# A hybrid token-mixer step: the scan is begun beside the last group's block inverse

## The chip, the cores and the metric

The kernel runs on one core of a Trainium2 chip. The metric is device time in microseconds (us) of one execution. TensorE (PE) does matrix products; VectorE (DVE), ScalarE (ACT) and GpSimd (POOL) work on tiles; SyncE (SP) issues most of the transfers, and ACT and POOL issue some. Each engine takes its instructions in order.

## The reference

One layer of a flow-matching backbone for 2048 sample tokens and 128 prompt tokens, D = 1024. The input is modulated and normalised, then projected once (`w_in`), and the columns are shared among three branches, which are gated and merged, and projected once more. The branch that the change touches is a gated DeltaNet, run in both directions:

```python
m = eye + bc[..., :, None] * jnp.einsum('bnhik,bnhjk->bnhij', kc, kc) * dec_strict
rhs = jnp.concatenate([vc * bc[..., None], kc * (bc * jnp.exp(gam))[..., None]], axis=-1)
sol = lax.linalg.triangular_solve(m, rhs, left_side=True, lower=True, unit_diagonal=True)
...
def step(s, inp):
    u0_, w_, qk_, qg_, kd_, gl_ = inp
    u = u0_ - jnp.einsum('bhck,bhkv->bhcv', w_, s)
    o = jnp.einsum('bhck,bhkv->bhcv', qg_, s) + jnp.einsum('bhij,bhjv->bhiv', qk_, u)
    s = gl_[..., None, None] * s + jnp.einsum('bhck,bhcv->bhkv', kd_, u)
    return s, o
```

The other branches are a spatial gating unit (SGU) and a Fourier mixer. All output is float32.

## The kernel before

Operands are split into a high and a low half-precision part, and each product is made of three matmuls (`mm3`, and `gemm_T` and `gemm_N` for the projections; all are recorded at L250, in the helper `mm`). Tokens are worked on in blocks of 512, 512, 512, 512 and 128 (`TBS`), or in 17 chunks of 128.

The stages follow one another on TensorE: modulation and normalisation; the columns for q, k and v with a short convolution; the SGU; the Fourier branch in four groups of columns, g = 0 to 3 (the projection, whose results are split into `xc` at L1571 and L1572; `columns_of`, `rows_in`, `rows_out`; the gates at L1454 to L1468, whose products `st` POOL makes at L1466 and stores at L1468); three merges, each with a gate and a branch projection for eight blocks of 128 output columns (L1690 loads the branch's blocks into `two`); and the output projection. Weights come through two buffers `wst`, loaded at L291 by SP.

The DeltaNet branch runs beside the SGU, the Fourier branch and the merges. It is a Python generator, `delta()`, that is advanced between pieces of the other stages: each piece adds to an account (`pace.tick`), and for each `QUOTA` of 1.6 units in it the generator goes on to its next `yield`. With scan the quota becomes `SCAN`. A unit is about a microsecond of TensorE's work. A scheduler then fixes each engine's order from the order of the code, from priorities and from its own estimate of times.

`delta()` does this:

- It prepares the 17 chunks one after another (`prep`), in five groups: [16], [0 to 3], [4 to 7], [8 to 11], [12 to 15]. The groups are numbered 0 to 4 here. For each chunk a triangular matrix is stored to DRAM (`nd`, issued by POOL at L1074).
- Beside the chunks of a group, `base_inverse` works on the group before it. It loads all 32x32 diagonal blocks of the group into `XB` (L1103), brings them into order with a copy on DVE (L1107), and inverts them in a chain of 31 steps. In each, DVE makes a product (L1114) and POOL subtracts it from `E` (L1115), and each waits for the other. ACT and DVE split the result in two (L1122, L1123), and it is stored to DRAM as `ei` of the group: groups 0 to 3 by SP at L1431 and by ACT at L1003; group 4 by SP at L1130 and by ACT at L1131.
- Group 4 has no chunks of another group beside it: it is worked on alone, to its end, in 27 slices.
- Then the pool `dqa` with all tiles of this part is closed, and a pool `dqb` takes its room. The tiles of the new pool cannot be written before the last readers of the old one have ended, stores included.
- `scan()` goes through 34 steps (chunk 16, then 0 to 15; and 16, then 15 to 0), some 12 slices each. A step's `level()` assembles the inverse of a chunk from its 32x32 blocks: it loads `ES` (L1171, three loads, from `ei`) and `N3` (L1175), both with one buffer, and `sn` (L1177); the first products are `ES` by `N3`; ACT and DVE split them into `Q3` (L1184 to L1186), POOL copies blocks from `ES` into `T16` and `R16` (L1188, L1190), and three more rounds of products follow. The buffers are cleared once by POOL (L1137). The chain of states S follows, with loads of `skn`, `sv`, `sk` and `sqk` (L1268 to L1322), and the output of a chunk (`attend`, `finish`: transposes at L1382, a store to `br`). Between its first loads and its first products scan lets 14 slices go by.

The merge of the DeltaNet branch is the last of the three, so that scan has until then to end.

## Time and profile before

| what | us |
|---|---|
| median of 3 runs (2136.2 to 2143.67) | 2139.85 |
| the profiled execution, its own time | 2138.49 |
| its span in the profile | 2136.7 |
| TensorE busy in the span | 2081.9 |

The granted clock of TensorE is 0.991 of full speed on average. In the rows below, a line such as L1114 is a line of the kernel before, and `out<-in` are the program's names without their buffer numbers. "SPq" is an engine's queue of transfers. A time in brackets behind an instruction is how long its engine had been idle, and what ended that. Where matmuls follow one another, a row gives the start of each and a length in which neighbours overlap.

### The profile page before, as it was taken

What the parts mean: (1) busy time and instruction counts of PE and PEld (TensorE: products, weight loads), DVE (VectorE), ACT (ScalarE), POOL (GpSimd) and SP (SyncE); (2) the same over time, 40 slices, a digit from 0 to 9 for tenths busy, and PEclk for the clock granted to TensorE, in tenths of its full rate; (3) what the DMA queues carried; (4) which work ended last, traced back from release to release, by engine and by line L of the source; (5) the groups of instructions that cost most, each with busy time, mean ns of one, the idle gap of its engine ahead of it and who ended that gap; (6) DMA issues with size and microseconds to landing.
All of it is one profiled execution on the core that took longest, in us unless ns stands there. A gap on an engine that the chain in (4) does not pass through costs nothing.

```text
span 2136.7 us, 42553 instructions
## 1 busy us (share of the span) xinstructions
PE 2081.9 (97%) x16133; PEld 1196.5 (56%) x16133; DVE 1326.9 (62%) x2945; ACT 1059.7 (50%) x2456; POOL 844.5 (40%) x1089
## 2 busy tenths in 40 slices
PE   7999999999999999989999999999999999999998
PEld 4454444455555678778565556565655444444443
DVE  6656854379777786556755555866665554666245
ACT  5554744465665664445644445765653443453112
POOL 0321332225465554543321233355542234333464
PEclk9999999999999999999999999999999999999999
DMA  9525722177767744444655555767764644456862
GB/s 354 221 78 188 271 103 103 62 222 232 254 222 247 217 162 133 110 133 128 228 178 168 168 162 185 236 203 233 210 207 131 218 163 165 173 193 236 343 221 89
DMA packets 222286, 403.24 MB, mean 189 GB/s; under 512 B 39225, under 2 KB 109137, under 8 KB 219265
## 3 DMA queue, kind: packets, MB, share of 16 engines
q1 hardware_dynamic: 167040, 290.58, 42.3%
q0 software_dynamic: 15216, 65.89, 8.2%
q10 hardware_dynamic: 39824, 44.05, 6.0%
q8 instruction: 127, 2.08, 0.4%
q14 instruction: 79, 0.64, 0.1%
HBM read 258.19 MB, written 142.24 MB: 187 GB/s over the span
## 4 chain that ended last, share of the span: by engine, by line
PE 53%; DVE 7%; DMA 5%; POOL 4%; ACT 3%; issue 3%; SPq 0%; ACTq 0%; POOLq 0%; DVEq 0%
PE b L250 52%; POOL E L1115 1%; DMA tw<-tw 1%; DVE XB L1114 1%; POOL st L1466 1%; DMA sqk<-qk 1%; DMA ei<-XB 1%; ACT nd L1066 0%; DMA wst<-in_w_blk_dram 0%; DVE XB L1123 0%; PE b L1382 0%; POOL ss L1024 0%; DMA br<-st 0%; DMA skn<-kv 0%; DVE xh L182 0%
## 5 line engine op out<-in xcount | busy, mean ns | idle before, releaser
L250 PE MATMUL b<-xh,whi 128*128 128x512 f16 (+1 forms) x1920 | 651.0, 348 | 1.7 <-DVE sg L1456 1.6
L250 PE MATMUL b<-xl,whi 128*128 128x512 f16 (+1 forms) x1920 | 651.1, 348 | 0.0
L250 PE MATMUL b<-xh,wlo 128*128 128x512 f16 (+1 forms) x1920 | 650.2, 347 | 0.0
L250 PEld LDWEIGHTS <-whi 128*128 128x128 f16 x3856 | 352.5, 98 | 324.8 <-issue 6.1
L250 PEld LDWEIGHTS <-wlo 128*128 128x128 f16 x1928 | 188.8, 98 | 175.8 <-issue 1.8
L250 PE MATMUL b<-big,bhi 128*128 128x512 f16 (+1 forms) x960 | 250.2, 347 | 0.1
L250 PE MATMUL b<-big,blo 128*128 128x512 f16 (+1 forms) x480 | 163.1, 347 | 0.0
L1739 POOL TENSOR_TENSOR mrow<-mrow,sg 128x512 f32<-128x512 f32 (+1 forms) x80 | 95.3, 1193 | 127.7 <-DVE sg L1738 103.4
L953 POOL TENSOR_TENSOR cy<-cy,raw 128x545 f32<-128x545 f32 (+1 forms) x48 | 65.5, 1390 | 182.7 <-ACT raw L952 182.7
L250 PEld LDWEIGHTS <-xh 128*128 128x128 f16 x1496 | 117.0, 98 | 29.0 <-issue 1.5
L250 PEld LDWEIGHTS <-bhi 128*128 128x128 f16 x960 | 87.5, 98 | 76.7 <-issue 0.2
L1115 POOL TENSOR_TENSOR E<-E,XB 128x31 f32<-128x31 f32 (+15 forms) x155 | 94.6, 610 | 85.3 <-DVE XB L1114 68.6
L250 PEld LDWEIGHTS <-xl 128*128 128x128 f16 x1068 | 98.1, 98 | 45.9 <-DMA tw<-tw 2.4
L1729 ACT ACTIVATE sg<-b,winv 128x512 f32<-128x512 f32 (+1 forms) x120 | 74.0, 617 | 93.4 <-PE b L250 92.4
L1188 POOL COPY T<-ES 32x256 f16<-32x256 f16 x68 | 31.9, 470 | 177.0 <-DMA ES<-ei 144.6
L250 PE MATMUL b<-whi,xh 128*128 128x128 f16 x544 | 92.8, 219 | 0.0
L250 PE MATMUL b<-whi,xl 128*128 128x128 f16 x544 | 92.8, 219 | 0.0
L250 PE MATMUL b<-wlo,xh 128*128 128x128 f16 x544 | 92.8, 219 | 0.0
L328 DVE SCALAR_TENSOR_TENSOR wlo<-wst,wsc,whi 128x1024 f16<-128x1024 f32 x52 | 71.0, 1368 | 30.2 <-ACT whi L327 29.0
L1295 POOL TENSOR_TENSOR skn<-skn,ed 128x512 f32<-128x512 f32 x34 | 37.1, 1090 | 112.6 <-DMA skn<-kv 112.6
L1114 DVE TENSOR_TENSOR XB<-XB,E 128x31 f32<-128x31 f32 (+15 forms) x155 | 54.3, 350 | 41.8 <-POOL E L1115 41.2
L315 ACT ACTIVATE wlo<-wst 128x1024 f16<-128x1024 f32 x52 | 54.8, 1055 | 50.5 <-DMA wst<-in_w_blk_dram 47.2
(531 smaller groups left out, 4315.0 us busy)
## 6 DMA issues: line engine op xcount, KB each, us to landing
wst<-in_w_blk_dram SPq DMA_DIRECT2D x58, 512.0 KB, 5.0
pa<-pa POOLq DMA_DIRECT2D x16, 896.0 KB, 4.6
qkv<-cy POOLq DMA_DIRECT2D x12, 1089.0 KB, 5.3
two<-br SPq DMA_DIRECT2D x24, 512.0 KB, 5.9
mrow<-mrg SPq DMA_DIRECT2D x16, 576.0 KB, 5.1
pa<-pa SPq DMA_DIRECT2D x5, 1792.0 KB
dc<-dec SPq DMA_DIRECT2D x17, 512.0 KB, 4.7
kq<-qkv SPq DMA_DIRECT2D x34, 256.0 KB, 4.7
```

The source lines that it names most:

```text
L250: newest[0] = PE.matmul(out, l, r, start=start, stop=stop, skip_group_check=reopened)
L315: w.squared = A.activation(w.lo, st, AF.Square, accum_out=ss)
L328: w.low = V.scalar_tensor_tensor(w.lo, st, s, w.hi, ALU.mult, ALU.subtract)
L953: G.tensor_tensor(y[:, c0:c1], y[:, c0:c1], raw[:, 1 + c0:1 + c1], ALU.mult)
L1114: V.tensor_tensor(t3, X3[:, 0:k, k:k + 1].to_broadcast([P, k, n_]), E3[:, k:k + 1, k:32].to_broadcast([P, k, n_]), ALU.mult)
L1115: G.tensor_tensor(E3[:, 0:k, k:32], E3[:, 0:k, k:32], t3, ALU.subtract)
L1188: G.tensor_copy(T16[rows(a0, b), :, :, b], ES[0:32, :, 2 * a0 + b, :, wT])
L1295: G.tensor_tensor(h3(kn_), h3(kn_), bc(ed[:, d, t, :], P), ALU.mult)
L1466: G.tensor_tensor(o, sg, src, ALU.mult)
L1729: gated_[0] = A.activation(sg, ps, AF.Sigmoid, scale=gw.inv)
L1739: G.tensor_tensor(mr, mr, sg, ALU.add)
```

## The change

Group 4's inverse gets a pool of its own, `lastp`, opened with the pool of the Fourier branch and closed with it; its room is used by the merges' pools afterwards. `delta()` issues group 4's loads (eight steps of the generator) and takes one slice for them, then closes `dqa`, opens `dqb` and begins scan. With every second slice of scan, group 4's inverse goes on by one step of its generator, which is two of its 31 steps. The first of its two stores for each half is issued by POOL instead of SP; ACT still issues the second. `SCAN` goes from 1.3 to 1.42.

```diff
-SCAN = 1.3
+SCAN = 1.42
...
-        XB = sb(dq, [P, 2048], "XB")
+        own = dq if g < 4 else lastp[0]
+        XB = sb(own, [P, 2048], "XB")
         X, tmp = XB[:, 0:1024], XB[:, 1024:2048]
-        E = sb(dq, [P, 1024], "E")
+        E = sb(own, [P, 1024], "E")
...
             else:
-                SY.dma_start(*out[0])
+                G.dma_start(*out[0])
                 A.dma_start(*out[1])
...
         for o_ in extra:
             SY.dma_start(*o_)
-        for _ in base_inverse(4):
-            yield 1
+        base = base_inverse(4)
+        for _ in range(8):
+            next(base)
+        yield 1
         dl.close()
         dq = pool(dl, "dqb", 1, side="right")
...
         pace.quota, pace.fine = SCAN, True
-        yield from scan()
+        for i_, _ in enumerate(scan()):
+            if i_ % 2:
+                next(base, 0)
+            yield 1
         dl.close()
...
     fp = pool(fs, "fp", 1)
+    lastp.append(pool(fs, "lastp", 1))
```

Lines behind L1093 move by one, and those of the Fourier branch and the merges by six or seven: L1114 is L1115 in the changed kernel, L1123 is L1124, L1456 is L1462, L1572 is L1579.

TensorE, in the second group of the Fourier branch, row 10871 on, before. `b_10081` is a projection's last tile; `xc_10043` is the split result of the one before it:

```order
10871 L250 MATMUL b_10081<-wlo_8406,xh_94 128x128
10872 L250 LDWEIGHTS xl_95
10873 L250 MATMUL b_10081<-whi_8405,xl_95 128x128
10874 L250 LDWEIGHTS xc_10043
10875 L250 MATMUL b_10109<-cf_1308,xc_10043 128x128
```

And now, where `b_10124` is the same projection:

```order
10871 L250 MATMUL b_10124<-wlo_8409,xh_94 128x128
10872 L250 LDWEIGHTS xl_95
10873 L250 MATMUL b_10124<-whi_8408,xl_95 128x128
10874 L250 LDWEIGHTS N_1229_9715
10875 L250 MATMUL b_10149<-ES_9717,N_1229_9715 128x32
```

The first products of scan stand in row 10875, behind the same projection and with as many rows ahead of them as the `xc` product had; before, they stood in row 12387.

DVE at the end of group 3's inverse, before (`XB_7998` and `E_7999` are group 3's; `sg` and `yT` belong to the Fourier branch's output, `xc_9671` to its next group):

```order
886 L1641 TENSOR_TENSOR yT_8301<-b_9397,us_9422 128x8x32
887 L1642 TENSOR_TENSOR yT_8301<-b_9397,us_9422 128x8x32
888 L1114 TENSOR_TENSOR XB_7998<-XB_7998,E_7999 128x60
889 L1456 SCALAR_TENSOR_TENSOR sg_9492<-b_9467,zs_8303,sg_9492 128x512
890 L264 CAST wscb_10126<-wss_10063 128x1
891 L1456 SCALAR_TENSOR_TENSOR sg_9561<-b_9536,zs_8303,sg_9561 128x128
892 L1114 TENSOR_TENSOR XB_7998<-XB_7998,E_7999 128x31
893 L1572 SCALAR_TENSOR_TENSOR xc_9671<-b_9574,xc_9671 128x512
894 L1123 SCALAR_TENSOR_TENSOR XB_7998<-E_7999,XB_7998 128x16x32 x4
```

And now (`XB_9692` and `E_9693` are group 4's, `xc_9674` is the tile that was `xc_9671`):

```order
886 L1108 COPY XB_9692<-XB_9692 64x1024
887 L1115 TENSOR_TENSOR XB_7998<-XB_7998,E_7999 128x60
888 L1462 SCALAR_TENSOR_TENSOR sg_9495<-b_9470,zs_8306,sg_9495 128x512
889 L1648 TENSOR_TENSOR yT_8304<-b_9400,us_9425 128x8x32
890 L1649 TENSOR_TENSOR yT_8304<-b_9400,us_9425 128x8x32
891 L1115 TENSOR_TENSOR XB_9692<-XB_9692,E_9693 128x31
892 L1115 TENSOR_TENSOR XB_7998<-XB_7998,E_7999 128x31
893 L264 CAST wscb_10187<-wss_10122 128x1
894 L1462 SCALAR_TENSOR_TENSOR sg_9564<-b_9539,zs_8306,sg_9564 128x128
895 L1115 TENSOR_TENSOR XB_9692<-XB_9692,E_9693 128x60
896 L1124 SCALAR_TENSOR_TENSOR XB_7998<-E_7999,XB_7998 128x16x32 x4
897 L1579 SCALAR_TENSOR_TENSOR xc_9674<-b_9577,xc_9674 128x512
```

Group 4's copy has moved ahead of group 3's last two steps, and the split of `xc` has moved behind group 3's four conversions. POOL's order moves with it: its three products `st` stand ahead of group 3's last step, where two steps stood behind them before; its clearing of scan's buffers stands behind six steps of group 4, and the other 25 stand between scan's copies.

More of the change, by code (lines that the diff above doesn't have):

```diff
@@ L1129, in base_inverse @@
             else:
-                SY.dma_start(*out[0])
+                G.dma_start(*out[0])
                 A.dma_start(*out[1])
-    odd, wide, q_st, q_hi = [1], [], [], []
+    odd, wide, q_st, q_hi, lastp = [1], [], [], [], []
     def zeroed(cols, tag):
```

## The prediction

> **What bounds the kernel now.** I read the page first, then TensorE's busy time by stretches of 10 us, then what it waited for in the stretches that stand out. The page's line of engines:
>
> ```profile
> PE 2081.9 (97%) x16133; PEld 1196.5 (56%) x16133; DVE 1326.9 (62%) x2945; ACT 1059.7 (50%) x2456; POOL 844.5 (40%) x1089
> ```
>
> TensorE is the bound, and the change takes no matmul away. So it can move the time only through TensorE's idle time and through the stretches in which its clock is granted at half. The stretches where that stands (start:end, length, then busy time by engine, granted clock, DMA share, GB/s):
>
> ```profile
> 890.00:900.00 10.00, 9.29 (x142) 8.06 (x140) 3.15 (x7) 3.40 (x8) 7.76 (x9) 1.00 0.83 243
> 900.00:910.00 10.00, 8.56 (x61) 4.31 (x59) 4.16 (x10) 3.45 (x6) 5.05 (x8) 1.00 0.49 144
> 910.00:920.00 10.00, 6.17 (x77) 5.10 (x74) 4.93 (x15) 4.62 (x14) 3.55 (x9) 0.75 0.32 85
> 920.00:930.00 10.00, 10.00 (x114) 7.07 (x112) 4.97 (x11) 4.16 (x12) 4.61 (x9) 0.91 0.36 116
> 930.00:940.00 10.00, 7.27 (x133) 6.83 (x131) 9.50 (x25) 5.15 (x15) 4.11 (x7) 1.00 0.67 197
> 1030.00:1040.00 10.00, 5.68 (x67) 4.77 (x63) 6.72 (x20) 8.36 (x21) 4.57 (x6) 0.72 0.81 275
> 1040.00:1050.00 10.00, 10.00 (x56) 4.78 (x55) 6.58 (x14) 6.13 (x13) 1.23 (x1) 0.94 0.91 329
> 1350.00:1400.00 50.00, 47.88 (x414) 27.96 (x413) 36.13 (x90) 34.14 (x91) 20.11 (x24) 1.00 0.77 237
> 1050.00:1650.00 600.00, 596.39 (x5302) 354.72 (x5301) 368.42 (x940) 318.76 (x837) 219.60 (x291) 1.00 0.62 191
> ```
>
> From 890 to 940 TensorE is idle for 0.71 + 1.44 + 3.83 + 2.73 = 8.7 us, and clocks of 0.75 and 0.91 cost 2.5 + 0.9 = 3.4 us more: 12.1 us. This is where scan begins. At 1030 to 1050, where the merges begin, the same reckoning gives 4.3 + 3.4 = 7.7 us. In the 600 us after that, through which scan runs on, only 3.6 us are idle. What TensorE waited for, first from 900 to 960, then from 1020 to 1060 (us in total, times, longest):
>
> ```profile
> PE b L250 <- DMA ES<-ei: 4.1, 2, 2.3
> PE b L250 <- DMA N<-n: 1.4, 1, 1.4
> PE b L250 <- ACT Q L1186: 1.0, 1, 1.0
> PE b L250 <- DVE X L1627: 0.8, 1, 0.8
> PE b L250 <- ACT R L1203: 0.5, 1, 0.5
> ```
>
> ```profile
> PE b L250 <- DVE Q L1219: 1.5, 1, 1.5
> PE b L250 <- DVE o L1248: 1.3, 1, 1.3
> PE b L250 <- DVE S L1232: 0.8, 1, 0.8
> PE b L250 <- ACT S L1231: 0.7, 1, 0.7
> ```
>
> The first list is scan's start: the loads of ES and N, which nothing has fetched ahead. SyncE's queue and the time line say why (start, us, engine, line, operation):
>
> ```profile
> SPq L1130 <- DVE XB L1123: 36.8, 1, 36.8
> ```
>
> ```profile
> 883.31 2.24 SPq L1130 DMA_DIRECT2D ei<-XB  x2
> 888.56 0.33 SPq L291 DMA_DIRECT2D wst<-in_w_blk_dram  x1
> 890.81 0.33 SPq L1270 DMA_DIRECT2D skn<-kv  x1
> 896.83 2.77 SPq L1171 DMA_DIRECT2D ES<-ei  x3
> ```
>
> ```profile
> 890.86 0.95 POOL L1137 MEMSET R<- 128x1024 f16 x1 [9.54 <-DVE Y L1572]
> 901.82 1.75 POOL L1188 COPY T<-ES 32x256 f16<-32x256 f16 x2 [3.19 <-DMA ES<-ei]
> ```
>
> ```profile
> 902.43 0.18 PE L250 MATMUL b<-ES,N 128*128 128x32 f16 x1 [1.44 <-DMA N<-n]
> 902.46 0.38 PE L250 MATMUL b<-xh,whi 128*128 128x512 f16 x1
> 902.67 0.28 PE L250 MATMUL b<-ES,N 128*128 128x32 f16 x5
> ```
>
> The store of group 4's inverse blocks SyncE for 36.8 us. When it has landed, near 890.8, its room goes to scan, and GpSimd's clearing and SyncE's loads begin together. The first product of scan comes at 902.43, **11.6 us after the landing**.
>
> **The change part by part.** The sum is made against the profiled execution, 2138.49 us, which is 1.4 us under the median of the three runs.
>
> *Scan's start leaves 900.* Scan's first room is now the one that group 3 frees. In the order, its first product stands in row 10875 of TensorE, where before the first `cf,xc` product of that place stood. This row gives the time of it:
>
> ```profile
> 838.13 0.28 PE L250 MATMUL b<-cf,xc 128*128 128x128 f16 x2
> ```
>
> So scan starts 64 us earlier on TensorE. Counted over the order's rows at 0.21 us for 512 columns (from 902.46 to 902.67 above), the first products of scan's steps now stand 22, 17, 18 and 19 us of TensorE's work apart, and stood 8.5, 10.7 and 7.3 apart. ES has one buffer, and one turn of clearing or freeing, loading and using it took the 11.6 us above: the old spacing is under that, the new one over it. The waits on ES and N go, and the weight load at 888.56, which was held up behind the store, is free. I take the whole 12.1 us off, and put 1.5 us back for the waits on ACT's Q and R, which are inside a step and come with it: **-10.6 us**.
>
> *Group 3's inverse ends later.* DVE now copies group 4's matrix ahead of group 3's last steps. The rows for it:
>
> ```profile
> 806.85 0.78 POOL L1074 DMA_DIRECT2D nd<-nd  x1 [0.68 <-ACT nd L1066]
> DMA to landing us min/median/max: 2.3/2.6/4.1
> 813.32 3.73 POOL L1466 TENSOR_TENSOR st<-sg,yT 128x512 f32<-128x512 f32 x3 [1.74 <-DVE XB L1114]
> 818.95 0.26 POOL L1115 TENSOR_TENSOR E<-E,XB 128x31 f32<-128x31 f32 x1
> 824.69 1.95 SPq L1431 DMA_DIRECT2D ei<-XB  x2
> 836.09 1.05 DVE L1107 COPY XB<-XB 64x1024 f32<-64x1024 f32 x1 [3.81 <-DMA XB<-nd]
> 824.03 0.28 PE L250 MATMUL b<-cf,xc 128*128 128x128 f16 x2
> ```
>
> (The second row is the landing time of the stores and loads of `nd`.) The store of 806.85 lands near 809.5; the load behind it takes up to 4.1 us, so near 814. DVE, in order, sits before the copy until then, copies for 1.05 us, does group 3's last step but one and two output products (near 817.2). GpSimd has put its three products of 3.73 us ahead of its last step, which therefore ends near 821.4 and not at 819.2. From that end to the store of 824.69, group 3's conversions took 5.5 us, so they now end near 826.9. DVE and ACT have them ahead of the split of `xc` (0.7 us more), which TensorE wants at 824.03: **a wait of 3.6 us** that was not there.
>
> *Scan's first room comes late.* The landing times of the stores and loads of `ei` from 800 to 905:
>
> ```profile
> DMA to landing us min/median/max: 5.3/5.7/5.9
> ```
>
> Group 3's second store went out at about 825.4, within the row of 824.69; it goes out 2.2 us later and lands up to 5.9 us after that, near 833.5. With the 11.6 us above the first product can begin at 845.2. TensorE gets there at 838.13 + 3.6 = 841.7: **another 3.6 us**. The two together put TensorE **7.2 us** back. Bounds: 2 us if DVE's copy comes in time, 11 us if GpSimd, which has six of group 4's steps ahead of the clearing, is late too. I take 7.2, since each term has its own row. While GpSimd waits for the landing, DVE waits with it for group 4's next step, and behind that stand splits of `xc`; TensorE wants these only after scan's first product, so they cost 0. So does the weight load that stands behind the same landing on SyncE, which is read later still.
>
> Behind these two waits the clock may fall to half. Between 910 and 920 it did after 3.8 us of idle time in several pieces. In 1350:1400, 2.1 us of idle time left it at 1.00. The new waits lie just short of the first. The Trainium skill, "TensorE: Matmul & The Clock Gate" (section "What's actually happening"), says that the clock falls to half after an idle window of about 3.4 us, and that the window runs free; by that rule one of the new waits can, but need not, hold a whole window. If the first does it, the second wait is filled by the slower work and the sum is unchanged. If the second does, it costs the 3.4 us of the two older cases; by that rule alone the sum would be 3.4 us higher at most. The trace agrees with it as far as it goes: both half-clock stretches follow idle time of about that size, though in pieces.
>
> *Group 4's inverse beside scan.* Its row in the stretch from 830 to 882 (ns, min/median/max):
>
> ```profile
> L1115 POOL TENSOR_TENSOR E<-E,XB x31: 247/587/1597, 837.5 to 880.0; 128x31 f32<-128x31 f32 x2, 128x60 f32<-128x60 f32 x2, 128x87 f32<-128x87 f32 x2, 128x112 f32<-128x112 f32 x2
> ```
>
> These 31 steps took 43 us with GpSimd nearly to themselves. Now 25 of them stand between scan's copies, which wait for loads. The order puts the last nine behind the fourth step's T copies, so that the store goes out some 60 us of TensorE's work after scan's start, and one ES load stands behind `two` on SyncE, which waits for that store. I count 2 to 3 us in hand: **0**; gone, it costs what the store is late beyond that. Two issues on GpSimd in place of SyncE cost 0.8 us each by the row of 806.85; GpSimd is 40% busy: 0.
>
> *The merges' start.* Scan's step there is another one, the crowd of operations the same. Bounds: -7.7 (all goes) to +3.4 (a second half-clock stretch). I take **-1.5**: one of the four waits above.
>
> *Wider steps.* 431 slices of 0.12 units more are 52 us of TensorE's work, against an earlier start of 42 (26 slices of 1.6) in the pace's units: the last step ends about 10 us later. By the order's rows scan's last transposes then stand 5 us of TensorE's work ahead of the last block that needs them, against 17 before. In the 600 us with 3.6 us idle the steps stand further apart. Bounds -3.6 to +3; I take **-1.5**.
>
> The sum: -10.6 + 7.2 + 0 - 1.5 - 1.5 = -6.4, so 2138.5 - 6.4 = **2132 us**. Against the median this is -0.37%. About 0.3%, 6.4 us, is what a measurement of this kernel can tell from no change: faster means under 2133.4.
>
> **The rivals.**
>
> *The gain is eaten on the way (same).* The new waits cost the clock (+3.4), and the merges give nothing back: -10.6 + 7.2 + 3.4 = 0, so 2138.5; with half of it, 2135. For it: two waits of 3.6 us only 14 us apart. Against it: the spacing of scan's steps removes the old waits in any case. Chance 0.33.
>
> *GpSimd's queue makes group 4 late (slower).* Each of the 25 steps waits behind scan's copies, which themselves wait for loads. If each takes 0.6 us longer, as long as one takes now, the store is 15 us late; less 2.5 in hand, TensorE waits 12.5 us at `two`'s ES load, with half clock 16: 2132 + 16 = 2148. It decides where TensorE loses 14 us to it, so from 13 us late on. For it: at its start scan's T copy has waited 3.2 us for ES (901.82). Against it: with the steps 17 us apart these loads are there early. The Trainium skill speaks for this rival ("Trainium Architecture — The Big Picture", section "What this means for kernel authors", which says that VectorE and GpSimd share a pair of ports as an exclusive lock): scan's two-input work on DVE would stretch group 4's steps on GpSimd. The maximum of 1597 ns against 587 in the row above may be such a case; 25 of them would be 25 us. Chance 0.15.
>
> *The change does more than I think (faster).* Group 3's end does not slip, and the merges' start is clean: -10.6 + 2 - 7.7 - 3 = -19, 2119. Chance 0.1, within "faster".
>
> **How the numbers follow.** The forecast has 0.42 and the better case 0.1, so faster has 0.52; same 0.33; slower 0.15. The likeliest case is 2132. The range goes from 2121, 2 us short of the better case, to 2144, midway between the eaten gain and the slower case: it leaves out half of the better case and nearly all of the slower one, some 0.2.
>
> **What would show it right or wrong.** Right: the waits on `ES<-ei` near 900 are gone and the clock there is 1.00; TensorE waits for `xc` near 824 and for ES or N near 842, 7 us together; the first product of scan begins near 845; SyncE has no wait of 36.8 us. Wrong: a half-clock stretch between 825 and 860; a wait of GpSimd for `XB` and of SyncE at `two` near 910; or waits on ES that are still there in scan's first four steps, which would mean that the spacing was not the cause.

## The result, and the profile after

| | before | after |
|---|---|---|
| median of 5 runs each, one chip, us | 2137.75 | 2151.12 |
| lowest and highest, us | 2133.26, 2143.67 | 2148.17, 2155.43 |
| the profiled execution, its own time, us | 2138.49 | 2148.17 |
| its span, us | 2136.7 | 2146.4 |

The ratio of after to before is 1.0064, with an interval of 1.0040 to 1.0088: the changed kernel is slower by 13 to 14 us, where a gain of 6 us was forecast. The profiled execution is the fastest of the five and shows 9.7 us of it. TensorE's line on the page after:

```profile
PE 2086.3 (97%) x16133; PEld 1197.9 (56%) x16133; DVE 1327.7 (62%) x2945; ACT 1060.5 (49%) x2456; POOL 850.0 (40%) x1091
```

The matmuls are as many as before (16133). TensorE's busy time grew by 4.4 us and its span by 9.7, so that the rest, 5.3 us, is idle time. Busy time can grow without more matmuls where the clock is lower, since each then takes longer. To see where, I cut the span where the kernel's work changes: 800 to 890 (the second group of the Fourier branch, where scan now begins), 890 to 960 (where scan began), 960 to 1020, 1020 to 1070 (the merges' start), 1070 to 1640 (scan runs on). Before, then after; the columns are those of the prediction's stretches:

```profile
800.00:890.00 90.00, 88.32 (x1172) 72.83 (x1172) 57.48 (x136) 41.36 (x88) 44.28 (x72) 0.97 0.38 109
890.00:960.00 70.00, 61.29 (x819) 48.53 (x817) 37.19 (x93) 30.07 (x76) 34.70 (x53) 0.95 0.49 148
960.00:1020.00 60.00, 58.62 (x845) 47.63 (x843) 39.05 (x106) 30.91 (x81) 20.47 (x37) 1.00 0.46 142
1020.00:1070.00 50.00, 45.68 (x365) 26.54 (x364) 37.00 (x96) 32.50 (x72) 18.93 (x25) 0.93 0.68 230
1070.00:1640.00 570.00, 566.39 (x5098) 339.12 (x5096) 345.85 (x886) 301.66 (x796) 211.15 (x281) 1.00 0.62 191
```

```profile
800.00:890.00 90.00, 81.75 (x1062) 65.70 (x1061) 54.78 (x133) 41.18 (x95) 54.25 (x86) 0.94 0.44 130
890.00:960.00 70.00, 64.54 (x870) 50.50 (x868) 46.40 (x120) 34.59 (x84) 25.36 (x46) 0.95 0.56 163
960.00:1020.00 60.00, 60.00 (x911) 51.35 (x909) 38.59 (x96) 30.48 (x75) 24.23 (x36) 1.00 0.43 134
1020.00:1070.00 50.00, 42.59 (x439) 28.34 (x437) 37.78 (x102) 31.91 (x78) 23.43 (x32) 0.90 0.65 210
1070.00:1640.00 570.00, 564.87 (x4952) 334.12 (x4951) 338.64 (x860) 293.18 (x760) 204.76 (x267) 1.00 0.60 186
```

Of each row, the length less PE's busy time is idle, and the length times what the clock lacks of 1.00 is lost to the clock. The two together, as the prediction reckoned them (us; the clock's two digits leave up to 0.5 us open in a row):

| stretch | before | after | difference | forecast |
|---|---|---|---|---|
| 800 to 890 | 1.7 + 2.7 = 4.4 | 8.2 + 5.4 = 13.6 | +9.2 | +7.2 |
| 890 to 960 | 8.7 + 3.5 = 12.2 | 5.5 + 3.5 = 9.0 | -3.2 | -10.6 |
| 960 to 1020 | 1.4 | 0.0 | -1.4 | 0 |
| 1020 to 1070 | 4.3 + 3.5 = 7.8 | 7.4 + 5.0 = 12.4 | +4.6 | -1.5 |
| 1070 to 1640 | 3.6 | 5.1 | +1.5 | -1.5 |
| sum | 29.4 | 40.1 | +10.7 | -6.4 |

The sum of the differences, 10.7, stands against 9.7 us of span; 4.2 of it go to the clock, about the 4.4 us by which TensorE's busy time grew. The last column has the prediction's terms. Its first term holds 1.5 us of waits for Q and R that move with scan's start, so by place it forecast +8.7 and -12.1. The new place costs about what was forecast, the old place gives back less than a third of what was forecast, and the merges' start costs where it should have gained. The waits of TensorE in the three places (us in total, times, longest), first from 805 to 880:

```profile
PE b L250 <- DVE sg L1462: 2.9, 1, 2.9
PE b L250 <- DMA N<-n: 2.2, 1, 2.2
```

then from 880 to 960:

```profile
PE b L250 <- DMA ES<-ei: 2.4, 1, 2.4
PE b L250 <- ACT S L1232: 1.0, 1, 1.0
```

and from 1020 to 1075:

```profile
PE b L250 <- ACT S L1232: 5.4, 2, 5.2
```

The first two are the two waits of the term +7.2. Their chain can be followed in the time line of the changed kernel:

```profile
813.89 1.03 DVE L1108 COPY XB<-XB 64x1024 f32<-64x1024 f32 x1 [2.19 <-DMA XB<-nd]
...
815.89 0.22 PE L250 MATMUL b<-whi,xh 128*128 128x128 f16 x1 [2.87 <-DVE sg L1462]
...
832.88 0.95 POOL L1138 MEMSET R<- 128x1024 f16 x1 [0.26 <-DMA ei<-XB]
...
843.75 0.46 PE L250 MATMUL b<-ES,N 128*128 128x32 f16 x8 [2.20 <-DMA N<-n]
```

DVE sits for 2.19 us before the copy of group 4 until its load has landed at 813.89, and TensorE waits for the `sg` product behind it. Group 3's store lands at 832.88; GpSimd then clears, SyncE loads, and the first product of scan comes at 843.75, 10.9 us after the landing. The second place, 880 to 960, in SyncE's queue and the time line:

```profile
SPq L1697 <- DMA ei<-XB: 5.4, 1, 5.4
```

```profile
912.75 0.84 POOL L1131 DMA_DIRECT2D ei<-XB  x1 [0.42 <-DVE XB L1124]
...
921.40 1.41 SPq L1697 DMA_DIRECT2D two<-br  x3
922.91 0.41 SPq L1273 DMA_DIRECT2D sv<-kv  x1
923.36 0.48 SPq L1172 DMA_DIRECT2D ES<-ei  x1
...
929.24 0.43 PE L250 MATMUL b<-ES,N 128*128 128x32 f16 x8 [2.38 <-DMA ES<-ei]
```

The 36.8 us wait of SyncE is gone, but the loads of `two` take the room of group 4's inverse and now wait 5.4 us for its store. The last of three ES loads stands behind them, goes out at 923.36, and TensorE waits for it. This is scan's fifth step; the first four begin at 843.75, 867.88, 888.91 and 907.53, and from the second on none waits for ES or N. The place cut at 920 and 940 shows it:

```profile
890.00:920.00 30.00, 30.00 (x485) 26.72 (x483) 19.52 (x46) 17.07 (x37) 12.79 (x25) 1.00 0.58 164
920.00:940.00 20.00, 16.13 (x120) 9.07 (x118) 10.13 (x28) 5.66 (x13) 4.71 (x8) 0.83 0.56 179
```

Up to 920, where the kernel before lost most of its 12.2 us, nothing is lost any more. From 920 to 940 it is 3.9 us of idle time and 3.4 of clock. The third place, first in SyncE's queue:

```profile
SPq L1273 <- DVE binv L1712: 10.6, 1, 10.6
```

```profile
1041.07 0.68 DVE L1233 SCALAR_TENSOR_TENSOR u<-sv,u 128x512 f16<-128x512 f32 x1
...
1041.77 0.32 SPq L1273 DMA_DIRECT2D sv<-kv  x1
...
1043.00 0.33 SPq L291 DMA_DIRECT2D wst<-in_w_brb_dram  x1
...
1046.35 0.63 ACT L315 ACTIVATE blo<-wst 128x512 f16<-128x512 f32 x1 [4.32 <-DMA wst<-in_w_brb_dram]
...
1049.90 0.61 ACT L1232 ACTIVATE S<-S 128x512 f16<-128x512 f32 x1
```

A load of `sv` holds SyncE's queue for 10.6 us, and the branch's weight load stands behind it. The view names `binv`, which came last, but `binv` does not touch `sv`; the buffer is read by DVE's u, which ends as the load goes out. ACT waits 4.32 us for the weights with its split of S behind that, and TensorE waits 5.2 us for S.

### The profile page after: what moved, and what is told of

It reads as the page before. It is cut to its first block, busy times and chain, and to the rows that moved or that the text cites. A ratio compares the mean times of both kernels' runs of the same rounds, so it can differ in the third digit from the quotient of the medians.

```text
span 2146.4 us, 42529 instructions
## 1 busy us (share of the span) xinstructions
PE 2086.3 (97%) x16133; PEld 1197.9 (56%) x16133; DVE 1327.7 (62%) x2945; ACT 1060.5 (49%) x2456; POOL 850.0 (40%) x1091
## 5 line engine op out<-in xcount | busy, mean ns | idle before, releaser
L327 ACT ACTIVATE whi<-wst,wsc 128x1024 f16<-128x1024 f32 x52 | 59.3, 1142 | 41.6 <-DVE wsc L278 41.6
L1115 DVE TENSOR_TENSOR XB<-XB,E 128x31 f32<-128x31 f32 (+15 forms) x155 | 56.2, 363 | 38.2 <-POOL E L1116 37.6
```

What stands on the lines that cost most here:

```text
L327: w.made = A.activation(w.hi, st, AF.Copy, scale=s)
L1115: V.tensor_tensor(t3, X3[:, 0:k, k:k + 1].to_broadcast([P, k, n_]), E3[:, k:k + 1, k:32].to_broadcast([P, k, n_]), ALU.mult)
```

## The experiments

The theory after the result (S in the expectations): the waits of scan's start were not removed by moving it. They went to the next place where a load comes late. Three were named above: scan's first products ahead of their room, and on SyncE's queue ES behind `two` and the weights behind `sv`. The rivals: the wider quota by itself is what costs; the place of the store's issue (GpSimd's queue) costs; group 4's chain beside scan costs wherever it stands. All ratios are to the kernel before on the same chip, with a 95% interval; its median was 2141.2 to 2141.9 us, so 0.1% is 2.1 us.

**The quota alone** (`e1_spacing_1_3`, the changed kernel; `e4_before_1_42`, the kernel before):

```diff
-SCAN = 1.42
+SCAN = 1.3
```

```diff
-SCAN = 1.3
+SCAN = 1.42
```

> The changed kernel with scan's quota back at 1.3; all else is as changed. Theory S (three separate places: group 3's late end and scan's late room near 820 to 850, 7 us; scan's fourth and fifth steps, where the ES load stands behind the load of two, 5 us with the half clock; the merges' start, 3 to 5 us): the first place stays, the second goes, since the order now has two behind the ES loads, the third depends on which slice falls there: 2139 to 2147. Rival W (the wider spacing itself is what costs): all of it comes back, 2130 to 2138. Rival G (GpSimd's queue with group 4's chain between scan's copies is what costs): nothing changes, 2148 to 2155.

> The kernel before with scan's quota at 1.42 and nothing else. Theory S: scan's start stays as it was, the spacing costs little but the merges' start falls on another step: 2132 to 2143. Rival W: 8 to 13 us more, 2146 to 2151. Rival G says nothing on it: as before, 2134 to 2142.

Measured: e1 2143.01 us, 0.9999 (0.9988 to 1.0010); e4 2157.02 us, 1.0061 (1.0049 to 1.0073). e1 lies in theory S's range, e4 above all three. With the old quota the changed kernel is as fast as the kernel before, and the kernel before with the new one loses as much as the change did. In e4 the loss lies at the end of scan, from 1640 to 1800 (first the stretch, then the wait):

```profile
1640.00:1800.00 160.00, 150.33 (x895) 75.11 (x893) 86.69 (x210) 69.51 (x153) 52.60 (x53) 0.96 0.52 175
```

```profile
PE b L250 <- DVE sg L476: 6.1, 1, 6.1
```

9.7 us are idle and 6.4 us go to the clock: scan ends too late for the last merge. The changed kernel, whose scan begins earlier, has PE busy through all of that stretch. So the wider quota needs the earlier start, but what the changed kernel loses is lost elsewhere. In e1 a trace shows how little the old quota cures by itself: its scan's start waits longer than in the changed kernel, from 805 to 890:

```profile
PE b L250 <- POOL T L1189: 5.5, 1, 5.5
```

Its profiled execution, 2147.16 us, was one of the slowest of its twelve, and by the same reckoning loses 41.1 us in the five stretches. Its gain of 9 us over the changed kernel, counted from the ratio of the repeat below, is thus measured but not located.

**Group 4's chain denser, or later** (`e2_every_slice`, `e3_start_later`, `e11_start_later_1_3`; changed kernel):

```diff
-            if i_ % 2:
+            if True:
```

```diff
-            if i_ % 2:
+            if i_ > 6:
```

The third has the second edit and `SCAN = 1.3`.

> The changed kernel with group 4's inverse going on at every slice of scan instead of every second. Theory S: the order puts two behind the ES loads of the fifth step, so the wait on ES near 930 and its half clock go (5 us); the waits near 820 and 842 and the merges' start stay as they are: 2143 to 2148. Rival W: no change, 2149 to 2154. Rival G: the chain stands more densely between scan's copies, so scan's first steps are later: 2151 to 2160.

> The changed kernel with group 4's inverse begun at scan's eighth slice and then going on at every slice. Theory S: DVE's copy for group 4 now stands behind group 3's conversions, so group 3 ends 2 us earlier, and two stands behind the ES loads: the wait for sg or xc near 815 to 827 (3 us) goes, the one for scan's first product shrinks by 2 us, that on ES near 930 goes: 2139 to 2145. Rival W: no change, 2149 to 2154. Rival G: 2149 to 2158.

> The third experiment with the quota at 1.3. Theory S: the spacing itself costs nothing, only where waiting loads fall: within 4 us of the third experiment, 2136 to 2144. Rival W (wider steps cost as such): 6 to 14 us less than the third, 2126 to 2134.

Measured: e2 2148.31 us, 1.0025 (1.0015 to 1.0035); e3 2140.31 us, 0.9991 (0.9981 to 1.0001); e11 2138.87 us, 0.9985 (0.9975 to 0.9995). A chain that begins at scan's eighth slice and then goes on with every slice (e3) takes 11 us off, counted from the lower of the changed kernel's two measurements (the repeat below); with every slice from the first on (e2) it is 4 us, the intervals overlap, and the time is just above theory S's range. In e3 group 4's copy is off DVE's queue while its load is under way: the wait for `sg` falls from 2.9 to 0.2 us. But TensorE then reaches scan's first product sooner and waits longer there. e3, from 805 to 880:

```profile
PE b L250 <- DMA N<-n: 4.2, 1, 4.2
```

So the two waits of the new place are one wait in two pieces; taking the first away lengthens the second from 2.2 to 4.2. By the same reckoning the new place still loses 13.6 us in e3; what it loses less is in 890 to 960, 3.1 us, where `two` waits only 1.2 us for the store. Between e3 and e11 the quota makes 1.3 us, inside the intervals.

**The store's queue** (`e5_store_on_sp`, changed kernel; `e12_room_store_sp` below):

```diff
-                G.dma_start(*out[0])
+                SY.dma_start(*out[0])
```

> The changed kernel with the first store of group 4's inverse back on SyncE's queue. Theory S (the time is lost at places where a load stands behind a waiting one on SyncE): the store now waits on SyncE for the conversions, with scan's loads of ES behind it, and two behind that still waits for its landing: the wait on ES near 925 stays or grows by up to 3 us: 2149 to 2157. Rival P (GpSimd's issue of the store holds up scan's copies behind it): that wait goes, 2142 to 2148.

Measured: 2149.55 us, 1.0042 (1.0030 to 1.0054). No difference from the changed kernel's 1.0064 (1.0040 to 1.0088) or its repeat below. That rival is out.

**The place at `two`** (`e9_two_behind_es`, changed kernel; `e13_two_behind_later`, the same with the mark one step later and `if i_ > 6 and i_ % 2`):

```diff
-            SY.dma_start(Ef[gi, 0:H * 512 - lo], eD[g][d, :, ci, lo:])
+            es = SY.dma_start(Ef[gi, 0:H * 512 - lo], eD[g][d, :, ci, lo:])
+            if d == 0 and t == 4:
+                mark[0] = es.ins
...
-            SY.dma_start(two, obD[n][2 * i:2 * i + 2, :, t0:t0 + tn].rearrange("g p t -> p g t"))
+            with tc.issue_after(mark[0]):
+                SY.dma_start(two, obD[n][2 * i:2 * i + 2, :, t0:t0 + tn].rearrange("g p t -> p g t"))
```

> The changed kernel with one thing moved: on SyncE's queue the first loads of two stand behind ES loads of the next step of scan, where the store that they wait for has long landed. Theory S: SyncE's wait of 5.4 us at two and TensorE's wait on ES of 2.4 us with the half clock behind it go: 5 to 8 us less than the changed kernel, 2143 to 2147. Rival D (the second experiment gained because the chain of group 4 ended at another place, not because of two): no change, 2149 to 2154.

> The ninth experiment (two behind the next step's ES loads) with group 4's inverse begun at scan's eighth slice, still at every second slice. DVE's copy for group 4 then stands behind group 3's conversions. Theory S: the wait for sg before 820 (2.9 us) goes and the first product's room is free earlier: 5 to 9 us less than the ninth, 2139 to 2143. Rival E (the third experiment gained this because the chain went on at every slice, not because it began later): no change against the ninth, 2146 to 2150.

Measured: e9 2148.07 us, 1.0030 (1.0018 to 1.0042); e13 2150.20 us, 1.0036 (1.0022 to 1.0050). In e9 both SyncE's wait at `two` and the ES wait from 880 to 960 are gone from the trace, and the stretch 890 to 960 loses 3.8 + 1.4 = 5.2 us, against 9.0 in the changed kernel. The median is 3 us under the changed kernel's two; by the ratios it is 3 and 7 us, and the intervals overlap. So the held load is worth some 3 to 4 us, and the other 5.2 us of that stretch have other causes. e13 shows that a later but not denser chain gains nothing beyond e9. Neither brings the gain that theory S expected.

**The changed kernel again** (`e14_changed_again`, no edit):

> The changed kernel, beside the kernel before on the same chip as the other two, so that the gain of the ninth and the thirteenth has a narrower interval. Theory S: 6 to 8 us over the ninth, 2152 to 2156 where before stands at 2141. Rival D (two's place on SyncE's queue is worth nothing): 2147 to 2150.

Measured: 2150.91 us, 1.0043 (1.0029 to 1.0057), with its profiled execution at 2145.05, again the fastest. The change costs 9 to 14 us. Here SyncE waits 5.8 us at `two` and TensorE 1.0 us for ES, and 890 to 960 still loses 8.6 us.

**The merges' start** (`e6_branch_weights_pool`: e3, and the branch's weights loaded by GpSimd):

```diff
-        load(st, src.rearrange("p (k c) -> p k c", c=cols))
+        if nkt == 4:
+            G.dma_start(st, src.rearrange("p (k c) -> p k c", c=cols))
+        else:
+            load(st, src.rearrange("p (k c) -> p k c", c=cols))
```

> The third experiment (group 4's inverse begun at scan's eighth slice, every slice) with the branches' weights loaded by GpSimd's queue instead of SyncE's. Theory S: at the merges' start the weight load no longer stands behind the load of sv, which waits for DVE's u; TensorE's wait on S at ACT (6.4 us) and the half clock behind it go: 7 to 10 us less than the third experiment, 2130 to 2134. Rival M (the merges' start is bound by the crowd on ACT and DVE itself): another wait takes its place, within 3 us of the third experiment, 2138 to 2143.

Measured: 2146.68 us, 1.0024 (1.0010 to 1.0037). This is outside both ranges. The longest wait for S there fell from 6.4 us in e3 to 1.8, and the stretch 1020:1070 loses 5.2 + 3.5 us in place of e3's 7.5 + 5.0. Still it is 6 us slower than e3: in its profiled execution 890 to 960 loses 6.5 + 4.9 us in place of 3.1, with waits for o and Q of scan's steps (3.1 and 1.9 us). Why these came with this edit is open.

The profiles of the other runs bear out this place. In seven of them (the changed kernel, its repeat, e2, e3, e5, e9 and e13) `sv` is held for 10.6 us or more with the branch's weights behind it, and 1020 to 1070 loses 11.5 to 15.2 us. In seven others (the kernel before, e4, e8, e10, e12, e16 and e18) the weights do not stand behind a held `sv`, and it loses 5.0 to 8.1. The other six lie between, 8.7 to 10.4 us.

**Own room without the earlier start** (`e8_own_room_only`, `e10_room_two_behind`, `e12_room_store_sp`; the kernel before with the new pool, group 4's inverse worked on to its end ahead of scan, quota 1.3):

```diff
-        XB = sb(dq, [P, 2048], "XB")
+        own = dq if g < 4 else lastp[0]
+        XB = sb(own, [P, 2048], "XB")
...
-        E = sb(dq, [P, 1024], "E")
+        E = sb(own, [P, 1024], "E")
...
-        for _ in base_inverse(4):
+        base = base_inverse(4)
+        for _ in base:
             yield 1
```

e8 has the store on GpSimd as the change has it, e12 on SyncE; e10 is e8 with `two` behind the ES loads of step `t == 3`.

> Only the room of its own and the store on GpSimd's queue: group 4's inverse is worked on to its end before scan begins, quota 1.3. The order now lets scan's clearing and first loads go ahead of group 4's end. Theory S: SyncE is not held for 37 us, so the first wait on ES or N near 900 goes; the spacing of scan's first steps is as before, so the second wait stays: 2132 to 2139. Rival N (nothing but the interleaving matters): as before, 2139 to 2144.

> The eighth experiment (own room, store on GpSimd's queue, group 4 worked on to its end before scan, 1.3) with the first loads of two behind the ES loads of a later step. Theory S: SyncE's wait of 12.3 us at two and TensorE's wait on ES of 5.7 us with its half clock go: 6 to 9 us less than the eighth, 2130 to 2134. Rival R (scan's first steps are too close for one ES buffer, so the wait only moves to the next load): 2137 to 2141.

> The eighth experiment with the first store of group 4's inverse on SyncE's queue, as before the change. Theory S: scan's first loads already stand ahead of the store, so SyncE's wait at the store takes the place of its wait at two and hides behind it: within 3 us of the eighth, 2137 to 2142. Rival P (the store's queue is what the eighth gained from): as the kernel before or slower, 2141 to 2147.

Measured: e8 2139.54 us, 0.9987 (0.9978 to 0.9996); e10 2140.58 us, 0.9997 (0.9987 to 1.0007); e12 2138.06 us, 0.9985 (0.9975 to 0.9994). The room alone gains 3 us, the queue of the store nothing. In e8 the block at the store is still there, at another load, from 840 to 960:

```profile
SPq L1693 <- DMA ei<-XB: 12.3, 1, 12.3
```

TensorE waits 5.7 us for ES behind it. e10 takes that load away and gains nothing, as its rival said: 890 to 960 loses 8.1 us in place of 9.9, now with waits for an output tile's store and for v (3.1 and 1.5 us).

**Scan later than its room** (`e7_scan_later_1_36`: e3, 1.36, and six slices ahead of scan; `e15_five_slices_1_3`, `e16_five_slices`, `e17_five_slices_1_3`, `e18_five_later_1_42`). The changed kernel lets one slice go by between the issue of group 4's loads and the closing of `dqa`. Here it is five:

```diff
-        yield 1
+        for _ in range(5):
+            yield 1
```

e16 has this edit alone; e17 has it and `SCAN = 1.3`; e18 has it and `if i_ > 6`; e15 has all three.

> The third experiment with six slices between group 4's loads and scan, and a quota of 1.36. Theory S: scan's first product stands 9 us of TensorE's work later, so that its room is free and its loads have landed: the wait on N near 842 (4 us) goes and the half clock behind it; the merges' start falls on another slice and stays a wait of some us: 2133 to 2139. Rival L (the first product's wait follows scan wherever it begins, since the loads start as late): no gain, 2139 to 2144.

> The eleventh experiment (begun later, every slice, 1.3) with five slices between group 4's loads and scan. Theory S: the wait of 5 us on N at scan's first product goes with its half clock, and nothing takes its place: 4 to 7 us less than the eleventh, 2131 to 2135. Rival L (the seventh experiment's outcome: other waits of scan's start and the merges take its place): 2137 to 2142.

> The changed kernel with one edit: five slices instead of one between the issue of group 4's loads and the start of scan. The quota stays 1.42, and group 4's chain still goes on from scan's first slices with every second one. Theory A (the first product stood ahead of the release of its room; four more slices of 1.6 units are some 6 us of TensorE's work, which is what the waits N 2.2 and 2.8 us with their half clock call for): the waits for N between 805 and 880 go and so does the half clock there, 9 to 11 us off the changed kernel's 2151: 2140 to 2142, ratio 0.999 to 1.001. Theory B (it needs the chain of group 4 to be later and denser): the sg wait of 2 to 3 us stays and the store of group 4 is late, since its chain ends later still; ratio 1.003 to 1.005.

> The changed kernel with two edits: the five slices of e16, and the quota back at 1.3. It differs from e15 only in group 4's chain (every second slice from the first on, where e15 has every slice from the eighth on). Theory A (room first, quota second): ratio 0.995 to 0.997, as e15. Theory B (the chain): ratio 0.999 to 1.000, like the changed kernel at 1.3 without the slices. In the order, the first loads of two stand ahead of the second step's ES here and behind the third step's in e15: if that decides, a wait on ES near 910 of about 2 us is left, ratio near 0.998.

> e15 with the quota at 1.42 instead of 1.3: five slices, and group 4's chain from the eighth slice of scan with every slice. Theory A (room first, quota second, chain no matter): as e16, 0.999 to 1.001. Theory B (the chain, quota no matter): as e15, 0.995 to 0.997. The order has the branch's weight load ahead of scan's sv load at the merges' start, as in the kernel before, so that ACT's wait there should be 1 us and not 5; if that place is what the quota costs, 0.997.

| kernel | median, us | ratio | interval |
|---|---|---|---|
| e7 | 2141.12 | 0.9994 | 0.9985 to 1.0003 |
| e16, five slices | 2139.46 | 0.9992 | 0.9981 to 1.0003 |
| e17, and quota 1.3 | 2134.88 | 0.9965 | 0.9951 to 0.9980 |
| e18, and the chain later | 2134.45 | 0.9969 | 0.9957 to 0.9981 |
| e15, and both | 2133.18 | 0.9957 | 0.9942 to 0.9972 |

Four more slices ahead of scan take the changed kernel from 1.0064 and 1.0043 to 0.9992, more than 10 us, with nothing else touched. With one of the other two edits it beats the kernel before by 7 us, and e15 by 9; e15, e17 and e18 cannot be told apart. Of the two theories, A has e16 and e17, and e18 goes against it. Five slices are no rule either: e7, with six and a quota of 1.36, is no faster than e3. Its wait for N is gone, but it waits 3.2 us for `sg` and loses 9.7 us at the merges' start. The waits and places of e16, first TensorE's from 805 to 860, then the time line:

```profile
PE b L250 <- DVE sg L1463: 2.7, 1, 2.7
```

```profile
852.37 0.21 PE L250 MATMUL b<-ES,N 128*128 128x32 f16 x2
...
924.99 0.37 SPq L1698 DMA_DIRECT2D two<-br  x1
925.45 1.34 SPq L1172 DMA_DIRECT2D ES<-ei  x3
...
1030.59 0.37 SPq L291 DMA_DIRECT2D wst<-in_w_brb_dram  x1
1034.40 0.46 SPq L1273 DMA_DIRECT2D sv<-kv  x1
```

All three places have changed with the one edit. The first product comes at 852.37 without a wait, where the changed kernel's stood at 843.75 behind 2.2 us of one. `two` is reached at 924.99 instead of 921.40 with no wait for the store left; the ES loads behind it are in time. And at the merges' start the weight load now stands ahead of `sv`. So this one edit is not a test of the first place alone. The stretches of e16, then three of e15 (rows left out are marked):

```profile
800.00:890.00 90.00, 84.89 (x1114) 69.64 (x1115) 58.50 (x140) 42.44 (x98) 56.08 (x90) 0.94 0.48 139
890.00:960.00 70.00, 69.25 (x1027) 57.43 (x1025) 53.65 (x130) 39.15 (x95) 34.08 (x56) 1.00 0.55 163
...
1020.00:1070.00 50.00, 44.99 (x411) 26.90 (x409) 42.30 (x102) 33.35 (x74) 16.18 (x20) 1.00 0.78 250
1070.00:1640.00 570.00, 560.19 (x4910) 330.94 (x4909) 328.87 (x850) 290.69 (x769) 202.82 (x273) 1.00 0.60 183
```

```profile
800.00:890.00 90.00, 87.60 (x1200) 72.07 (x1201) 60.92 (x148) 44.56 (x105) 56.18 (x89) 0.96 0.49 145
890.00:960.00 70.00, 62.23 (x834) 48.69 (x832) 49.60 (x130) 36.23 (x89) 30.37 (x53) 0.95 0.58 177
...
1070.00:1640.00 570.00, 568.74 (x4978) 336.82 (x4977) 338.44 (x871) 297.64 (x790) 203.49 (x269) 1.00 0.61 192
```

By the same reckoning as above (lost us in one profiled execution of each):

| stretch | before | after | after again, e14 | e16 | e17 | e18 | e15 |
|---|---|---|---|---|---|---|---|
| 800 to 890 | 4.4 | 13.6 | 10.4 | 10.5 | 9.5 | 4.2 | 6.0 |
| 890 to 960 | 12.2 | 9.0 | 8.6 | 0.8 | 6.8 | 0.7 | 11.3 |
| 1020 to 1070 | 7.8 | 12.4 | 11.7 | 5.0 | 10.3 | 6.9 | 10.4 |
| 1070 to 1640 | 3.6 | 5.1 | 5.5 | 9.8 | 0.3 | 12.2 | 1.3 |

The first row says that scan's room was not what e16 gained by: with its first product free of a wait it still loses 10.5 us there, as the changed kernel's repeat does (10.4). It waits 2.7 us for `sg`, and 5.4 us go to the clock. Only where the chain begins later as well (e18, e15) does that place fall to 4.2 and 6.0. What e16 gains against the repeat lies in the next two rows, 7.8 and 6.7 us, and 4.3 of it are lost again after 1070.

With the quota of 1.42 and five slices (e16, e18) the old place loses 0.8 and 0.7 us, where 12.2 were lost before: the forecast's -10.6 is there, and more. The 570 us after the merges' start then lose 9.8 and 12.2 us; the largest waits there are for DVE's u (4.2 and 4.5 us) and S (2.2 and 2.7) of scan's own steps. With 1.3 (e17, e15) it is the other way round: 6.8 and 11.3 us in the old place, and 0.3 and 1.3 us afterwards. The four sums lie between 24 and 29 us. Which slice meets which piece of the Fourier branch and the merges differs between them, and that this sets where the loss falls is argued, not shown.

Four pairs of kernels with the early start differ in the quota alone: the changed kernel and e1 by 9 to 14 us, e16 and e17 by 6, e18 and e15 by 3, e3 and e11 by 1, the last two inside the intervals. In none is 1.42 faster.

## Why the prediction was wrong, point by point

**Scan's start leaves 900, -10.6: this step failed.** It held that the waits on ES and N "go", and with them the whole 12.1 us, because scan's steps stand 17 us and more of TensorE's work apart and one turn of the ES buffer takes 11.6. Its reason held for four steps: the start moved to the predicted row, the 36.8 us wait went, and 890 to 920 loses nothing. But the old place as a whole gave back 3.2 us, since 9.0 are lost from 920 to 960. The distance between steps on TensorE says when the next load is wanted, not when it can be issued. At the fifth step ES stands behind a load of `two` that waits 5.4 us for group 4's store, TensorE waits 2.4 us for ES, and the clock costs 3.4 to 3.5 us there. e9, without that held load, puts its share at 3 to 4 us; the rest is in short waits inside scan's steps (S and X 1.0 each, u 0.5) and in the clock, and no run separates it. That `two` is not all of it shows in e15 and e6 too, where it does not wait for the store and the stretch loses 11.3 and 11.4 us.

**Group 4's inverse beside scan, 0: wrong in size.** The prediction saw that an ES load stands behind `two` and counted 2 to 3 us in hand. SyncE was held for 5.4 us, and TensorE waited 2.4 and then ran with a clock of 0.95 over the stretch. It is the slower rival's place at a small part of its price: the steps on GpSimd took no longer beside scan's work. The group of them from 830 to 882 before, and from 810 to 912 in the changed kernel (busy time, mean ns of one, idle time ahead):

```profile
L1115 POOL TENSOR_TENSOR E<-E,XB 128x31 f32<-128x31 f32 (+15 forms) x31 | 17.6, 569 | 25.5 <-DVE XB L1114 24.5 <-DVE wsc L277 0.5 <-DVE wscb L264 0.4
L1116 POOL TENSOR_TENSOR E<-E,XB 128x135 f32<-128x135 f32 (+15 forms) x36 | 20.5, 571 | 25.2 <-DVE XB L1115 24.4 <-DVE winv L325 0.4
```

The mean of 571 ns (five steps of group 3 are in it) stands against 569 before. By the ports that the Trainium skill names there ("Trainium Architecture — The Big Picture", section "What this means for kernel authors") it could have grown, and the trace does not show it; but DVE was no busier beside these steps than before (54.8 us of 800 to 890, before 57.5). TensorE lost a few us and not 16. e9 puts the held load at 3 to 4 us, so the rival did not make the result; that its 2148 lies near it is chance.

**The two new waits, +7.2: right, a little low.** 9.2 us were lost there, against 8.7 with the waits for Q and R that move along. The landing of group 4's load, "near 814", came at 813.89; the landing of group 3's store, "near 833.5", at 832.88; the first product, "845.2", at 843.75. The first wait is at `sg`, which stands some rows ahead of `xc` on DVE, and not at `xc`; it is shorter (2.9 for 3.6), and so is the second (2.2 for 3.6). What the term missed is the clock, 5.4 us in place of 2.7 in that stretch; the prediction had set up to 3.4 us for it in the range.

**The merges' start, -1.5: wrong in sign.** It lost 4.6 us more. The rows of before showed four short waits, and I took one of them off; the term leaves out which loads stand ahead of the weights on SyncE once scan's step there is another one. In e16 and e18, where the weight load stands ahead of `sv` again, the stretch loses 5.0 and 6.9 us, less than before. The profiles above go the same way. e6 moved that load off the queue; the place lost less than e3's (8.7 for 12.5), and the whole did not gain. So the order accounts for this place's loss in the main, and taking it away is not shown to be a gain by itself.

**Wider steps, -1.5: wrong in sign.** In none of the four pairs is 1.42 faster; the ratios put its cost at 1 to 14 us, twice inside the intervals. After 1070, 1.5 us more are lost in the changed kernel, and e16 and e18 lose 9.8 and 12.2 in all, against 0.3 and 1.3 with 1.3 and the same five slices. The prediction had the bound at +3 only. That the wider quota is affordable only with an earlier start was right: the kernel before pays 16 us for it at scan's end (e4).

**The chances.** The forecast had the gain and the losses fall in separate places and added them; the slower case had 0.15 and one mechanism. What happened is the middle rival's pattern, a gain eaten on the way, carried further: -3.2 in place of -10.6, and only 1.4 us back elsewhere (960 to 1020). Of the prediction's three signs of being wrong two came, the half clock between 825 and 860 and SyncE's wait at `two`; the third, a wait on ES in the first four steps, did not, which speaks for the spacing.

**Left open.** What the rest of the old place's loss comes from, beyond the held load; why e1 measures 9 us under the changed kernel while its profiled execution loses as much; why e6 loses more from 890 to 960; and whether e15's three edits add up, as e15, e17 and e18 lie within each other's intervals.

## What to carry to other kernels

When work is moved earlier, it meets other work, and every queue that it uses gets a new order at more places than the one that the change is about. Here four slices more ahead of scan (by the expectation some 6 us of TensorE's work) were the difference between 0.4 to 0.6% slower and no loss, and in the profiles most of that lay 70 and 200 us behind the place that they were meant for. On an in-order queue of transfers a blocked load is not removed by giving its buffer to another user; list what will be the next one to block and what stands behind it, at every place where the order changes. And where two edits are joined, such as an earlier start and a wider spacing, measure each by itself: the earlier start with the old quota cost nothing, and with five slices it gained 0.3 to 0.4%.

## What the runs showed of the hardware

Half clock followed idle time that was shorter than the 3.8 us of the prediction's case, and not always. In the changed kernel the wait of 2.9 us at 815.89 left the clock at 1.00, and the wait of 2.2 us at 843.75 was followed by half clock. In its repeat (e14) it was the other way round: half clock followed a wait of 2.3 us for `sg` (0.83 from 810 to 820), and a wait of 2.8 us at scan's first product left it at 1.00. PE is busy for all of 830 to 840 in both; the next stretch, after and then e14:

```profile
840.00:850.00 10.00, 7.80 (x66) 4.84 (x64) 4.40 (x13) 4.78 (x10) 4.67 (x9) 0.83 0.59 165
```

```profile
840.00:850.00 10.00, 7.22 (x63) 4.22 (x61) 4.72 (x13) 4.45 (x9) 4.65 (x9) 1.00 0.50 159
```

A clock of 0.83 over 10 us is 1.7 us lost, as much as 3.4 us at half clock lose. The time line of the changed kernel shows the fall, 1.3 us after TensorE has begun to work again:

```profile
844.82 0.43 PE L250 MATMUL b<-xh,whi 128*128 128x512 f16 x1
845.04 0.63 PE L250 MATMUL b<-xl,whi 128*128 128x512 f16 x1
845.47 0.63 PE L250 MATMUL b<-xh,wlo 128*128 128x512 f16 x1
```

Up to 845.04 these products begin 0.22 us apart, from there on 0.43. The Trainium skill, "TensorE: Matmul & The Clock Gate" (section "What's actually happening"), names an idle window of about 3.4 us that runs free. The free run agrees with the two executions, since the same place falls or does not; the length does not, as 2.2 and 2.3 us of idle time were enough here, so the measurement decides. That this is part of why single executions of one kernel lie several us apart (2145.05 to 2155.43 us for the changed kernel in its two sets of runs) is likely, and not shown.
